# Three buffers for transposed x and five for the output, in a batched matrix product

## The chip, the cores and the metric

The kernel runs on one core of a Trainium2 chip. The metric is the device time of one execution in microseconds (us), less is better; eight runs of the kernel before are shown. One further view is the profile of one execution: its span runs from the first to the last instruction, and its own time is given beside it.

## The reference

32 independent products of a 256x512 matrix by a 512x384 matrix, inputs and output in float32:

```python
def reference(x, y):            # x: 32 x 256 x 512, y: 32 x 512 x 384
    return np.einsum('bij,bjk->bik', x, y).astype(np.float32)
```

x is 16.8 MB, y is 25.2 MB, the output is 12.6 MB: 54.5 MB pass between memory and the core in each execution, whatever the order.

## The kernel before

The 32 products are cut into 8 groups of 4 (`Q = 4`); n numbers the groups from 0 to 7. The product is made in float16 with float32 sums. The work of one group consists of these parts, named by the letters of the text `PLAN`:

- **x**n and **y**n: the loads, issued by SP. x arrives as one transfer of 2 MB, y as one of 3 MB; y7 comes in four quarters. `x_pool` and `y_pool` hold two buffers each, so x(n) waits until VectorE has read x(n-2), and y(n) until it has read y(n-2).
- **T**n: VectorE casts x to float16 (`x_r`, one buffer, line 100) and transposes it in 32x32 blocks into `xt_sb` (line 107: two instructions per group, four for groups 6 and 7).
- **R**n: VectorE casts y to float16 in four pieces (line 113).
- **M**n: TensorE, 128 matmuls in two halves of 64 (line 126). A half fills four PSUM tiles; the pool has eight, so each half of M(n) needs the four tiles of the same half of M(n-1) to have been copied out.
- **C**n and **D**n: the copies from PSUM to the output tile `o_sb` (line 147), by ScalarE (C) and VectorE (D). For groups 0 to 5 ScalarE makes 28 copies and VectorE 4, the last four of the group; for group 6 ScalarE makes all 16 (of 64 partitions), for group 7 the two share 8 and 8.
- **S**n: the store, issued by SP (line 156); for groups 6 and 7 in two halves, here called S6a, S6b, S7a, S7b.

`PLAN` writes the parts out in program order, and `keep_in_program_order` makes each engine follow it. SP, too, issues its transfers in that order: a transfer whose condition isn't met holds up those behind it.

```python
PLAN = """
x0 x1 y0
T0 x2 y1
T1 R0 M0 C0 x3 y2
T2 D0 R1 M1 C1 x4 y3 S0
T3 D1 R2 M2 C2 x5 y4 S1
T4 D2 R3 M3 C3 x6 y5
T5 D3 R4 M4 C4 x7 y6 S2
T6 D4 R5 M5 C5 y7
T7 D5 R6 M6 C6 R7 M7 C7 D7 S3 S4 S5 S6 S7
"""
```

VectorE thus does, for a middle group, T(n), D(n-2), R(n-1). With two buffers of `xt_sb`, the transposes of T(n) write where M(n-2) reads, so they wait for the end of M(n-2), and D(n-2) and R(n-1) stand behind them. With six buffers of `o_sb`, the copies of group 6 wait for the store S0 and those of group 7 for S1.

Of the kernel before, what the change touches and what calls it, by code (L numbers as in the profile page):

```python
# [1 line left out]

# [4 lines left out]


MM_DT = mybir.dt.float16
F32 = mybir.dt.float32  # L10
P = 128


Q = 4
STEP = 4
O_BUFS = 6
WIDE_GROUPS = 6


# [15 lines that stand above are left out]
@with_exitstack  # L35
def kernel(
    ctx: ExitStack,
    tc: tile.TileContext,
    x: bass.AP,
    y: bass.AP,  # L40
    out: bass.AP,
):
    nc = tc.nc

    B, I, J = x.shape
    _, _, K = y.shape

    PQ = P // Q
    R = I // PQ
    T = J // PQ  # L50
    TW = T // 2
    NE = I // P
    N = B // Q

    x_pool = ctx.enter_context(tc.tile_pool(name="x_pool", bufs=2))
    y_pool = ctx.enter_context(tc.tile_pool(name="y_pool", bufs=2))
    xr_pool = ctx.enter_context(tc.tile_pool(name="xr_pool", bufs=1))
    xt_pool = ctx.enter_context(tc.tile_pool(name="xt_pool", bufs=2))
    yr_pool = ctx.enter_context(tc.tile_pool(name="yr_pool", bufs=2))
    o_pool = ctx.enter_context(tc.tile_pool(name="o_pool", bufs=O_BUFS))  # L60
    psum_pool = ctx.enter_context(
        tc.tile_pool(name="psum", bufs=2 * Q, space=bass.MemoryType.PSUM)
    )

    keep = tc.keep_in_program_order

    x_of, y_of, xt_of, yr_of, ps_of, o_of = {}, {}, {}, {}, {}, {}  # L70

    def width(n):
        return PQ if n < WIDE_GROUPS else 2 * PQ

    def on_vector(n, e, g):
        if n < WIDE_GROUPS:
            return (e, g) == (NE - 1, Q - 1)
        return n == N - 1 and g % 2 == 1

    def load_x(n):  # L80
        x_of[n] = x_pool.tile([P, R, J], F32, name="x_sb")
        keep(
            nc.sync.dma_start(
                out=x_of[n],
                in_=x[n * Q : (n + 1) * Q].rearrange("g (p r) j -> (g p) r j", r=R),
            )
        )

    def load_y(n):
        y_of[n] = y_pool.tile([P, T, K], F32, name="y_sb")  # L90
        src = y[n * Q : (n + 1) * Q].rearrange("g (q t) k -> (g q) t k", t=T)
        step = STEP if n == N - 1 else T
        for a in range(0, T, step):
            keep(nc.sync.dma_start(out=y_of[n][:, a : a + step], in_=src[:, a : a + step]))

    def transpose_x(n):


        x_r = xr_pool.tile([P, R, J], MM_DT, name="x_r")
        keep(nc.vector.tensor_copy(x_r, x_of.pop(n)))  # L100
        xt_of[n] = xt_pool.tile([P, NE, TW, P], F32, name="xt_sb")
        b = width(n) // PQ
        src = x_r.bitcast(F32).rearrange("p (b h e) (q t) -> p b e t h q", b=b, e=NE, t=TW)
        dst = xt_of[n].rearrange("p e t (h s b) -> p b e t h s", s=PQ, b=b)
        for e in range(NE):
            for c in range(b):
                keep(nc.vector.transpose(dst[:, c, e], src[:, c, e]))  # L107

    def round_y(n):
        y_sb = y_of.pop(n)  # L110
        yr_of[n] = yr_pool.tile([P, T, K], MM_DT, name="y_r")
        for a in range(0, T, STEP):
            keep(nc.vector.tensor_copy(yr_of[n][:, a : a + STEP], y_sb[:, a : a + STEP]))  # L113

    def multiply(n):
        xt = xt_of.pop(n).bitcast(MM_DT).rearrange("p e t (m c) -> p e t m c", c=2)
        y_r = yr_of.pop(n)
        o_of[n] = o_pool.tile([P, R, K], F32, name="o_sb")
        for e in range(NE):
            for g in range(Q):  # L120
                ps_of[n, e, g] = psum_pool.tile([P, K], F32, name="o_ps")
            for t in range(T):
                for g in range(Q):
                    s = slice(g * PQ, (g + 1) * PQ)
                    keep(
                        nc.tensor.matmul(  # L126
                            ps_of[n, e, g],
                            xt[s, e, t // 2, :, t % 2],
                            y_r[s, t],
                            start=(t == 0),  # L130
                            stop=(t == T - 1),
                        )
                    )

    def collect(n, vector):
        w = width(n)
        per = P // w
        copy = nc.vector.tensor_copy if vector else nc.scalar.copy
        o = o_of[n].rearrange("p (u f) k -> p u f k", u=Q // per)
        for e in range(NE):  # L140
            for g in range(Q):
                if on_vector(n, e, g) != vector:
                    continue
                ps = ps_of.pop((n, e, g))
                a = g % per * w
                for h in range(per):
                    keep(copy(o[a : a + w, g // per, h * NE + e], ps[h * w : (h + 1) * w]))  # L147

    def store(n):
        w = width(n)  # L150
        per = P // w
        o = o_of.pop(n).rearrange("p (u f) k -> p u f k", u=Q // per)
        for u in range(Q // per):
            b = n * Q + u * per
            keep(
                nc.sync.dma_start(
                    out=out[b : b + per].rearrange("g (s f) k -> (g s) f k", s=w),
                    in_=o[:, u],
                )
            )  # L160

    parts = {
        "x": load_x,
        "y": load_y,
        "T": transpose_x,
        "R": round_y,
        "M": multiply,
        "C": lambda n: collect(n, False),
        "D": lambda n: collect(n, True),
        "S": store,  # L170
    }
    for step in PLAN.split():
        parts[step[0]](int(step[1:]))


# [1 line left out]
_INS = ['x', 'y']  # L177
_OUTS = [((32, 256, 384), 'float32')]


# [23 lines left out]
```

## Time and profile before

| what | value |
|---|---|
| median of 8 runs | 136.37 us (135.37 to 136.85) |
| the profiled execution's own time | 136.85 us |
| its span | 135.1 us |
| VectorE busy | 95.5 us (71%) |
| ScalarE busy | 91.7 us (68%) |
| TensorE matmul busy | 58.7 us (43%), mean granted clock 0.802 |
| moved by the SP queue | 54.53 MB, 95.9% of 16 DMA engines' span |

The profiled execution is the longest of the eight shown, 0.48 us over their median.

Every transfer with the time of its issue and of its landing, both in us from the start of the span (the trace gives issue and time to landing; the sum is the landing). A transfer has landed when its last DMA engine is done:

| transfer | issued | landed | | transfer | issued | landed |
|---|---|---|---|---|---|---|
| y1 | 11.2 | 33.8 | | y6 | 84.6 | 103.1 |
| x3 | 17.1 | 38.7 | | S2 | 85.1 | 106.9 |
| y2 | 24.4 | 45.9 | | y7, first quarter | 99.0 | 108.7 |
| x4 | 27.9 | 51.2 | | y7, second | 99.4 | 110.6 |
| y3 | 39.7 | 59.3 | | y7, third | 100.0 | 112.5 |
| S0 | 40.7 | 62.9 | | y7, fourth | 100.7 | 114.3 |
| x5 | 41.9 | 67.9 | | S3 | 101.4 | 117.9 |
| y4 | 54.2 | 75.2 | | S4 | 102.1 | 121.6 |
| S1 | 55.2 | 78.8 | | S5 | 115.4 | 125.2 |
| x6 | 56.4 | 83.7 | | S6a | 122.6 | 127.0 |
| y5 | 69.9 | 90.9 | | S6b | 124.6 | 130.5 |
| x7 | 72.1 | 95.8 | | S7a | 128.5 | 132.3 |
| | | | | S7b | 129.6 | 134.0 |

How to read it: a row of the page's strip has 40 slices of the span, with the busy share in tenths. "Idle before" is time in which an engine did nothing, and the name behind the arrow is what ended it. The DMA share is a mean over 16 engines: it can be under one while some of them are still full.

### The profile page before, as it was taken

How to read it: one execution, taken by the hardware profiler on the slowest of the kernel's cores; microseconds unless marked ns; L12 is line 12 of the kernel's file. 1: busy time of each engine (PE TensorE's matmuls, PEld its weight loads, DVE VectorE, ACT ScalarE, POOL GpSimd, SP SyncE). 2: the span in 40 equal slices, each digit the busy share in tenths (PEclk: the TensorE clock that was granted, in tenths of full speed). 3: DMA queues.
4: the chain of work that ended last, by engine and by line, in shares of the span. 5: the costliest groups of instructions: out<-in, count | busy, mean ns of one | idle time of the engine just before them, and what ended most of it. 6: DMA issues, size and time to landing. Idle time of an engine off the chain costs nothing.

```text
span 135.1 us, 2452 instructions
## 1 busy us (share of the span) xinstructions
PE 58.7 (43%) x1024; PEld 34.5 (26%) x1024; DVE 95.5 (71%) x92; ACT 91.7 (68%) x193; POOL 0.2 (0%) x4
## 2 busy tenths in 40 slices
PE   0000005970099006970099106930499007977700
PEld 0000003540056004540056003610255004634400
DVE  0049999649993899629993899769990999904530
ACT  3000000099997999499986999799958999599720
POOL 0000000000000000000000000000000000000000
PEclk9999999999559955599559955995558965899965
DMA  5999999999999999999999999999999999998774
GB/s 121 422 442 454 408 434 422 442 458 391 456 434 398 429 425 446 346 423 439 444 451 393 418 452 420 444 400 446 449 415 403 404 424 440 422 434 353 313 306 171
DMA packets 4187, 54.68 MB, mean 405 GB/s; under 512 B 464, under 2 KB 464, under 8 KB 1488
## 3 DMA queue, kind: packets, MB, share of 16 engines
q1 hardware_dynamic: 4176, 54.53, 95.9%
q8 instruction: 8, 0.13, 0.4%
q14 instruction: 3, 0.02, 0.0%
HBM read 41.94 MB, written 12.58 MB: 404 GB/s over the span
## 4 chain that ended last, share of the span: by engine, by line
DVE 43%; PE 39%; DMA 6%; ACT 5%; issue 3%; DVEq 0%
PE o_ps L126 39%; DVE xt_sb L107 23%; DVE o_sb L147 11%; DMA x_sb<-in_x_dram 6%; DVE y_r L113 5%; ACT o_sb L147 5%; DVE x_r L100 3%; DVEq L199 0%
## 5 line engine op out<-in xcount | busy, mean ns | idle before, releaser
L147 ACT COPY o_sb<-o_ps 32x384 f32<-32x384 f32 (+1 forms) x192 | 90.4, 471 | 36.8 <-PE o_ps L126 32.7
L126 PE MATMUL o_ps<-y_r,xt_sb 32*128 32x384 f16 x1024 | 58.7, 394 | 68.6 <-DVE y_r L113 66.8
L126 PEld LDWEIGHTS <-xt_sb 32*128 32x128 f16 x1024 | 34.5, 112 | 92.5 <-issue 57.8
L107 DVE STREAM_TRANSPOSE xt_sb<-x_r 128x1024 f32<-128x1024 f32 (+1 forms) x20 | 31.5, 1621 | 16.7 <-PE o_ps L126 16.7
L113 DVE CAST y_r<-y_sb 128x1536 f16<-128x1536 f32 x32 | 28.4, 953 | 0.2
L100 DVE CAST x_r<-x_sb 128x4096 f16<-128x4096 f32 x8 | 18.3, 2288 | 9.7 <-DMA x_sb<-in_x_dram 9.7
L147 DVE COPY o_sb<-o_ps 32x384 f32<-32x384 f32 (+1 forms) x32 | 17.8, 556 | 7.5 <-PE o_ps L126 6.9
L147 ACT ACT_TABLE_LOAD x1 | 1.3, 1283 | 0.7 <-PEq L188 0.7
L188 POOL MEMSET const-bfloat16-1.0<- 128x1 bf16 x1 | 0.1, 103 | 0.0
L188 POOL MEMSET const-uint8-127<- 128x1 uint8 x1 | 0.1, 102 | 0.0
L188 POOL MEMSET const-float32-0.0<- 128x1 f32 x1 | 0.1, 100 | 0.2 <-issue 0.2
L188 POOL MEMSET const-float32-1.0<- 128x1 f32 x1 | 0.1, 99 | 0.0
## 6 DMA issues: line engine op xcount, KB each, us to landing
y_sb<-in_y_dram SPq DMA_DIRECT2D x7, 3072.0 KB, 21.0
x_sb<-in_x_dram SPq DMA_DIRECT2D x8, 2048.0 KB, 22.5
out_dram<-o_sb SPq DMA_DIRECT2D x6, 1536.0 KB, 20.6
y_sb<-in_y_dram SPq DMA_DIRECT2D x4, 768.0 KB, 11.8
out_dram<-o_sb SPq DMA_DIRECT2D x4, 768.0 KB, 4.4
```

The costliest lines, as they stand in the source:

```text
L100: keep(nc.vector.tensor_copy(x_r, x_of.pop(n)))
L107: keep(nc.vector.transpose(dst[:, c, e], src[:, c, e]))
L113: keep(nc.vector.tensor_copy(yr_of[n][:, a : a + STEP], y_sb[:, a : a + STEP]))
L126: nc.tensor.matmul(ps_of[n, e, g], xt[s, e, t // 2, :, t % 2], y_r[s, t], start=(t == 0), stop=(t == T - 1),)
L147: keep(copy(o[a : a + w, g // per, h * NE + e], ps[h * w : (h + 1) * w]))
L188: nc = _bacc.Bacc("TRN2", target_bir_lowering=False, num_devices=1)
```

## The change

Two numbers. The pool of transposed x gets a third buffer, the pool of output tiles loses its sixth. No instruction is added, removed or moved on any engine. With three buffers T(n) waits for the end of M(n-3) in place of M(n-2). With five output buffers, the copies of group 5 wait for S0, those of group 6 for S1, those of group 7 for S2.

```diff
-O_BUFS = 6
+O_BUFS = 5
...
-    xt_pool = ctx.enter_context(tc.tile_pool(name="xt_pool", bufs=2))
+    xt_pool = ctx.enter_context(tc.tile_pool(name="xt_pool", bufs=3))
```

## The prediction

> **What bounds the kernel now.** I read the strip of slices and the queues first, then VectorE's waits, then ScalarE's order of time, and last the transfers of the end.
>
> The page's strip and its queues:
>
> ```profile
> DMA  5999999999999999999999999999999999998774
> GB/s 121 422 442 454 408 434 422 442 458 391 456 434 398 429 425 446 346 423 439 444 451 393 418 452 420 444 400 446 449 415 403 404 424 440 422 434 353 313 306 171
> ...
> q1 hardware_dynamic: 4176, 54.53, 95.9%
> q8 instruction: 8, 0.13, 0.4%
> ```
>
> From the second slice to the 36th, 3 to 121 us, the DMA engines are full at some 425 GB/s; only the last four slices show room. The table of transfers says the same: landings follow each other in the order of issue, at distances that are the sizes over one rate. S0 to x5 is 5.0 us for 2.10 MB, x5 to y4 7.3 us for 3.15 MB, y4 to S1 3.6 us for 1.57 MB: 420 to 437 GB/s. Every one had been issued 8 us or more before its predecessor landed, S0 to y7 alike. The transfers are one line that never runs dry up to S4 at 121.6 us; an earlier issue lengthens the line and lands nothing earlier.
>
> VectorE's waits:
>
> ```profile
> DVE xt_sb L107 <- PE o_ps L126: 16.7, 6, 3.8
> DVE x_r L100 <- DMA x_sb<-in_x_dram: 9.7, 2, 8.5
> DVE o_sb L147 <- PE o_ps L126: 6.9, 2, 5.3
> ```
>
> The first row is the wait at issue: six transposes, T2 to T7, wait 16.7 us in all for the matmuls two groups earlier, at most 3.8 us each.
>
> ScalarE in order of time (start, duration, idle before):
>
> ```profile
> 86.31 13.56 ACT L147 COPY o_sb<-o_ps 32x384 f32<-32x384 f32 x28 [0.63 <-PE o_ps L126]
> 101.79 13.56 ACT L147 COPY o_sb<-o_ps 32x384 f32<-32x384 f32 x28 [1.92 <-PE o_ps L126]
> 116.71 9.80 ACT L147 COPY o_sb<-o_ps 64x384 f32<-64x384 f32 x20 [1.35 <-issue]
> 127.25 1.95 ACT L147 COPY o_sb<-o_ps 64x384 f32<-64x384 f32 x4 [0.74 <-PE o_ps L126]
> ```
>
> A block is the 28 copies of a group, 13.56 us. The idle times before blocks 1 to 5 are 0.94, 1.79, 1.57, 0.63 and 1.92, together 6.85 us: behind VectorE stands an engine with much less room than 16.7 us.
>
> The end, in stretches (columns: length, then busy time and count for PE, weight loads, VectorE, ScalarE, GpSimd; clock, DMA share, GB/s):
>
> ```profile
> 118.00:121.40 3.40, 2.45 (x55) 1.35 (x51) 0.07 (x1) 3.28 (x8) 0.00 (x0) 1.00 1.00 417
> 121.40:125.00 3.60, 2.77 (x64) 1.64 (x60) 1.55 (x3) 3.47 (x8) 0.00 (x0) 1.00 0.88 370
> 125.00:129.00 4.00, 2.35 (x57) 1.44 (x49) 2.34 (x5) 3.17 (x8) 0.00 (x0) 1.00 0.65 260
> 129.00:135.10 6.10, 0.00 (x0) 0.00 (x0) 0.56 (x1) 0.19 (x1) 0.00 (x0) 0.53 0.64 262
> ```
>
> Up to 134.0, the last landing, the 16 engines are idle for a mean of 0.12x3.60 + 0.35x4.00 + (5.0 - 0.64x6.10) = 0.43 + 1.40 + 1.10 = 2.9 us. Those engines wait for S6 and S7, which are issued late because the copies are late. But the last landing is that of the slowest engine. The transfers between 126 and 130 us, in steps of 0.1 us:
>
> ```profile
> GB/s 246 614 184 553 184 369 553 471 492 369 369 246 492 123 307 246 246 184 0 62 61 61 61 61 0 61 0 61 0 0 61 0 61 799 184 492 430 430 492 123
> ...
> q8 instruction: 1, 0.02, 1.6%
> ```
>
> From 127.9 to 129.3 one packet (61 GB/s is 6 KB in 0.1 us) follows another: nearly all engines have run dry and one still works on S6b. In the same stretch stands one packet of instructions, 1.6% of 16 engines for 4 us, so 1.0 us of one engine. Since S4, landings follow at 3.6 (S5), 1.8 (S6a), 3.5 (S6b), 1.8 (S7a) and 1.7 us (S7b). A half store takes 1.8; S6b took 1.7 us more, though it was issued at 124.6, 2.4 us before S6a landed. S7a was issued at 128.5, again before S6b landed. So the slowest engine had work all the time: in this execution the end was set by its line of transfers, lengthened by 1.7 us, and not by the copies.
>
> **The change, part by part.**
>
> The third xt buffer. All six waits go. T2 starts at 27.9 in place of 29.83; D0 and R1 behind it come 1.9 us earlier. What is late next: the second half of M1 needs the PSUM tiles of M0's second half, which ScalarE copies until 40.69, so M1 still ends near 44. The gain reaches ScalarE only as its idle time: 0.94 us before block 1. After that blocks 2 to 4 can follow each other: 27.13 + 4x13.56 = 81.4 for block 4, in place of 86.31. It also needs y4, landed 75.2, plus 6 us (cast 1.0, then half of M4, 4.2 to 5.3 between M and C in the rows), 81.2. From there the loads decide. x6 lands at 83.7; cast 2.29, transposes 4.03 and D4 2.26 bring R5 to 92.3 (before 95.38). Its first piece 0.97, wake-up 0.14 and the half of M5 5.3: block 5 starts at 98.7 and ends at 112.3 in place of 115.36. Block 6 follows at once: 112.3 in place of 116.71, 4.4 us earlier. The y7 quarter that landed at 114.3 ends its cast at 115.3; M7's halves are freed by block 6, so C7, D7 and the issues of S6a, S6b, S7a, S7b come 4.4 us earlier: 118.2, 120.2, 124.1, 125.2. S5 is issued at 112.3.
>
> What that is worth: the line of transfers from S4, landed 121.6, then never runs dry on any engine. S5 125.2, S6a 127.0, S6b 128.8, S7a 130.6, S7b 132.4. Before, 134.0. The gain is 1.6 us if the extra at S6b goes, and 0 if the instruction packet again delays the engine that ends last, since that engine never had a gap to close. The busy shares give a farthest bound of 2.9 us, if all 16 engines end together.
>
> Is the packet's engine fixed? No row tells. I take the value without the repeat, since a full line leaves only the slowest engine's bad luck to matter, and since the profiled run, 0.48 over the median, looks like one with the delay. Both ends stay in the range. The sum: 136.85 - 1.6 = 135.25. Against the median this is a gain of 1.1 us: without the delay, a run of before would be held by the copies instead (S7b issued 129.6 plus 3.5 to 4.0 us), about 0.5 us lower than the profiled one, which is where the median lies.
>
> The Trainium skill, "Perfetto Trace Analysis", section "Optimization Strategy", says that the same gap repeated on the engine that should be saturated can mean too few buffers for the next tile. VectorE's six gaps fit, and by that reading alone the sum would be 136.85 - 16.7 = 120.2; the filled DMA rows contradict it. "DMA: Bandwidth & Descriptors", section "Where 436 GB/s comes from", puts the ceiling of the 16 ports at 435.2 GB/s: my estimate from it is 54.53 MB / 435.2 = 125.3 us for the transfers alone, which speaks against any large gain; the sum by it would end no earlier than about 127 us, and the measured distances of landings are what I use.
>
> The output buffer. C5 newly waits for S0, landed 62.9, and starts no earlier than 98: slack 35 us. C6 waits for S1 (78.8) and starts at 112: slack 33. C7 and D7 wait for S2, landed 106.9; they start at about 118: slack 11 us. S2 stands behind y6 on SP's queue, and y6 is issued earlier, not later. The DVE copy D5 waits for S0 as well, with R6, R7 and D7 queued behind it: it too is 35 us clear. Cost 0; if S2's cover were gone, C7, M7's PSUM and S7 would slip by whatever S2 exceeded 118.
>
> SP's queue: x4 and later loads are issued up to 5 us sooner, none behind a new wait. TensorE: M stays in bursts at clock 0.5 to 1.0; both halves of M7 at the slow rate (a half took 2.8 us in the tail at clock 1.00, 5.3 in M5) would add 5.0 us to S7b, which would be issued at 130.2, still before its turn in the line at 130.6.
>
> **The rivals.**
>
> 1. The delay recurs: the slowest engine ends at 134.0 again. For: it was full throughout. Against: eight instruction packets over 16 engines need not fall there. Time 136.4 to 136.85.
> 2. The copies were the true bound: the end moves with them by 4.4 us, to 132.4. For: the chain of waits ends in matmuls and copies. Against: S5, S6b and S7a landed at the pace of the line, not of their issue.
> 3. Slower: instruction packets fall twice on the engine that ends last, in place of once. Its price is 1.0 us by the row above, at the last store: 137.9. It decides from the second packet on; with only the one it is rival 1. For: nothing but chance and a line without gaps in which to catch up. Against: the number of instructions is unchanged.
>
> **How the numbers follow.** Forecast 0.50 (own range 134.4 to 135.7), rival 1 0.34, rival 2 0.03, rival 3 0.09, the rest, unnamed losses, 0.04. The median moves by over 0.5%, 0.68 us, in the forecast and rival 2: faster 0.52 with a little taken for gains that come out small; rival 1 is within 0.5%, 0.36; slower 0.12. A difference of 0.5% is about what a measurement of this kernel can tell from none. The range, 134.2 to 136.9, takes in the forecast and rival 1, and most of the 2.9 us bound.
>
> **What would show it.** VectorE's wait of line 107 for TensorE gone; ScalarE's idle before blocks 1 to 5 down from 6.85 to 2 us or less; VectorE's wait for x landings up from 9.7; landings up to S4 within 0.5 us of the table; S7b issued near 125 and landing some 7 us later; DMA share near 1 until 130. I am wrong if landings before S4 move, if a copy waits for a store, or if the last landing stays at 134.

## The result, and the profile after

The changed kernel is faster: ratio to the kernel before 0.9942, with a 95% interval of 0.9917 to 0.9968. Its median is 135.25 us (135.07 to 135.93, 12 runs), against 136.21 us for the kernel before in the same comparison (135.19 to 137.63, 33 runs). The ratio is taken over fast runs alone (those not over 1.5% above the fastest of their kernel); the quotient of the two medians is 0.993. The profiled execution took 135.93 us at a span of 134.1 us, against 136.85 and 135.1.

The page's strip and queues of the changed kernel:

```profile
DMA  5999999999999999999999999999999999999991
GB/s 112 420 435 445 432 418 430 459 432 403 452 413 447 403 449 425 355 425 419 474 408 393 435 449 452 423 403 435 427 440 401 409 425 443 420 414 423 417 385 55
...
q1 hardware_dynamic: 4176, 54.53, 96.5%
```

The room in the last four slices (8, 7, 7, 4 before) is gone: the engines are full to the 39th slice. The stretches of the end (length, busy time and count of PE, weight loads, VectorE, ScalarE, GpSimd; clock, DMA share, GB/s):

```profile
121.40:125.00 3.60, 1.86 (x45) 1.08 (x37) 1.93 (x5) 2.79 (x7) 0.00 (x0) 1.00 0.97 404
125.00:129.00 4.00, 0.00 (x0) 0.00 (x0) 0.47 (x1) 0.10 (x1) 0.00 (x0) 0.58 1.00 418
129.00:134.10 5.10, 0.00 (x0) 0.00 (x0) 0.00 (x0) 0.00 (x0) 0.00 (x0) 0.50 0.38 159
```

Between 125 and 129 us the DMA share is 1.00 where it was 0.65, while no matmul is left and hardly a copy: the computation is over and the stores are still draining.

The waits of the changed kernel, all engines:

```profile
DVE x_r L100 <- DMA x_sb<-in_x_dram: 19.8, 5, 8.6
...
DVE y_r L113 <- DMA y_sb<-in_y_dram: 3.2, 4, 0.9
```

The row of the transposes waiting for TensorE (16.7 us before) has no successor here. In its place VectorE waits 19.8 us for x, where it was 9.7, and 3.2 us for y, which it never waited for before. ScalarE in order of time:

```profile
27.04 54.32 ACT L147 COPY o_sb<-o_ps 32x384 f32<-32x384 f32 x112 [25.04 <-PE o_ps L126]
82.51 13.56 ACT L147 COPY o_sb<-o_ps 32x384 f32<-32x384 f32 x28 [1.15 <-PE o_ps L126]
99.03 23.38 ACT L147 COPY o_sb<-o_ps 32x384 f32<-32x384 f32 x48 [2.95 <-issue]
123.16 1.95 ACT L147 COPY o_sb<-o_ps 64x384 f32<-64x384 f32 x4 [0.74 <-PE o_ps L126]
```

The blocks of groups 0 to 3 follow each other without a gap (112 copies in 54.32 us); the gaps that are left stand before group 4 and group 5, where the loads are late. The last copies on ScalarE start 4.1 us earlier, 123.16 for 127.25. And the last store, issue and then time to landing:

```profile
125.54 0.42 SPq L156 DMA_DIRECT2D out_dram<-o_sb  x1
```

```profile
out_dram<-o_sb SPq DMA_DIRECT2D x1, 768.0 KB, 7.6
```

The same store in the kernel before:

```profile
129.63 0.33 SPq L156 DMA_DIRECT2D out_dram<-o_sb  x1
```

```profile
out_dram<-o_sb SPq DMA_DIRECT2D x1, 768.0 KB, 4.4
```

S7b is issued 4.1 us earlier and takes 7.6 us to land, where it took 4.4. Of 4.1 us that the copies won, the end keeps 0.9 (133.1 for 134.0).

### The profile page after: what moved, and what is told of

It reads as the page before. It is cut to its first block, busy times and chain, and to the rows that moved or that the text cites. A ratio compares the mean times of both kernels' runs of the same rounds, so it can differ in the third digit from the quotient of the medians.

```text
span 134.1 us, 2449 instructions
## 1 busy us (share of the span) xinstructions
PE 61.5 (46%) x1024; PEld 35.4 (26%) x1024; DVE 96.3 (72%) x92; ACT 91.7 (68%) x193; POOL 0.2 (0%) x4
## 4 chain that ended last, share of the span: by engine, by line
DMA 42%; DVE 20%; PE 16%; ACT 13%; issue 1%; DVEq 0%
DMA x_sb<-in_x_dram 42%; PE o_ps L126 16%; ACT o_sb L147 13%; DVE xt_sb L107 7%; DVE x_r L100 7%; DVE o_sb L147 5%; DVE y_r L113 1%; DVEq L199 0%; DVEq L100 0%
## 5 line engine op out<-in xcount | busy, mean ns | idle before, releaser
L126 PE MATMUL o_ps<-y_r,xt_sb 32*128 32x384 f16 x1024 | 61.5, 400 | 61.7 <-DVE y_r L113 49.3
L126 PEld LDWEIGHTS <-xt_sb 32*128 32x128 f16 x1024 | 35.4, 113 | 87.4 <-issue 53.4
L100 DVE CAST x_r<-x_sb 128x4096 f16<-128x4096 f32 x8 | 18.4, 2294 | 19.9 <-DMA x_sb<-in_x_dram 19.8
```

Of the source, the lines that this page charges most:

```text
L126: nc.tensor.matmul(ps_of[n, e, g], xt[s, e, t // 2, :, t % 2], y_r[s, t], start=(t == 0), stop=(t == T - 1),)
```

## The experiments

Two theories are told apart. By the **line theory** the end is the end of one full line of transfers, and what the copies win beyond it waits in that line. By the **copies theory** the end is the last copy plus a fixed time for its store.

### Each half of the change, and fewer output buffers

```diff
# e1: kernel before
-O_BUFS = 6
+O_BUFS = 5
# e2: the change itself
# e3: the change, and
-O_BUFS = 5
+O_BUFS = 4
# e4: the change, and
-O_BUFS = 5
+O_BUFS = 3
```

> Only the second half of the change: two buffers of xt_sb as before, five of o_sb in place of six. Line theory (the one line of transfers sets the end, and the third xt buffer is what keeps it full at the end): the new waits are for stores that landed long ago, S0 at 63, S1 at 79 and S2 at 107 us, against copies that start at 102, 117 and 121: no change, within 0.3% of before, and T2 to T7 still wait 16 to 17 us for TensorE. Rival (the smaller output pool costs or gains something of its own): over 0.5% from before in either direction.

> The whole change once more, beside the others on the same chip. Line theory: 0.4 to 0.9% faster than before, S7b issued near 125.5 and landing 7 to 8 us later, at 133. Rival (the copies set the end): the last landing follows the issue of S7b by under 5 us.

> Three buffers of xt_sb, four of o_sb. C7 and D7 now wait for S3, which landed at 118.6 in the changed kernel, while C7 started at 116: a delay of 2.5 to 3 us, so S7b is issued near 128.5 in place of 125.5. Line theory: S7b's turn in the line begins only near 131.3, so the time is that of the change, within 0.3%. Copies theory: the whole delay shows, 2 to 2.5% slower than the change.

> Three buffers of xt_sb, three of o_sb. C6 waits for S3 (landed 118.6, C6 started 112.6) and C7 for S4 (122.2): the copies of group 6 are late by 6 us, those of group 7 by 6 to 7, S7b is issued near 132. Line theory: the slack of the copies, about 5 us, is used up, and the end slips by what exceeds it and the 3.5 us that a half store takes from issue to landing: last landing 135 to 136, 1 to 2% slower than the change, about 1% slower than before. Copies theory: 6 us, 4.5% slower than the change. If the output buffers never matter: equal to the change.

| run | median us | ratio to before | interval | S7b issued | S7b landed |
|---|---|---|---|---|---|
| e1, five output buffers alone | 136.33 | 0.9984 | 0.9946 to 1.0022 | 129.6 | 133.6 |
| e2, the change | 135.32 | 0.9931 | 0.9900 to 0.9961 | 124.8 | 132.6 |
| e3, xt three, output four | 135.34 | 0.9911 | 0.9883 to 0.9939 | 124.5 | 132.6 |
| e4, xt three, output three | 140.15 | 1.0277 | 1.0237 to 1.0317 | 133.0 | 137.0 |

e1: no effect of the output half shows, within 0.4% either way; S7b is issued at 129.56, where it was 129.63, and VectorE's wait stays:

```profile
DVE xt_sb L107 <- PE o_ps L126: 16.4, 6, 3.7
```

e1 and e3 together put the gain on the third xt buffer: with it, five and four output buffers are equal within their intervals. (Three xt and six output buffers together were not run; e9 below has the gain with six output buffers.)

In e3 the wait that I expected didn't appear. I had taken C7 to start at 116, but ScalarE is busy with group 6 until about 119.4, and S3 landed at 118.1. So e3 says nothing on the slack of the copies.

e4 does, though its wait fell earlier than I had put it. With three buffers C5 waits for S2, which landed at 106.5. ScalarE in e4:

```profile
82.54 13.54 ACT L147 COPY o_sb<-o_ps 32x384 f32<-32x384 f32 x28 [2.17 <-issue]
106.56 23.34 ACT L147 COPY o_sb<-o_ps 32x384 f32<-32x384 f32 x48 [10.48 <-DMA out_dram<-o_sb]
```

Its gap of 10.48 us ends with a store. Group 5 starts at 106.56, against 98.33 in e2, 8.2 us late; S7b is issued 8.2 us late too, and the last landing is only 4.4 us late (137.0 for 132.6), the time 4.8. The change thus has some 3.8 us in which copies may be late at no cost, which is 132.6 less the 124.8 of the issue and the 4.0 that S7b needs when only S7a is ahead of it. Neither theory's own number (1 to 2%, or 4.5%) was met against the change, 3.6%: there is slack, as the line theory has it, but 3.8 us of it in place of about 5, and the delay was larger than I had worked out.

### A store less, more copies

In e5 and e6 one store is never issued, in the changed kernel and in the kernel before; in e7 and e8 eight copies of group 6 are made twice.

```diff
# e5 (change), e6 (before): in store(n)
+        if n == 3:
+            return
# e7 (change), e8 (before): in collect(n, vector)
-                for h in range(per):
+                for h in range(per) if (n, e) != (6, 0) else [*range(per)] * 2:
```

> The changed kernel with the store S3 left out: the output of group 3 is never written, so 1.57 MB less pass through the line, 3.6 us by the distances of landings; every copy is still made. Line theory: S7b, issued near 125.5, gets its turn at 127.7 in place of 131.3; the last landing comes 3 to 3.6 us earlier, 2.2 to 2.7% faster than the change, about 3% faster than before. Copies theory: nothing changes, since no copy waits for S3.

> The kernel before with the store S3 left out (the output of group 3 is never written). Here S7b is issued at 129.6 and cannot land before about 133.3, whatever the line. Line theory with the copies just behind: 0 to 0.9 us faster than before, at most 0.7%, a quarter or less of what the same cut gives the changed kernel. If the line alone had set the end of before: 3 us or more, over 2%.

> The changed kernel with the eight copies of the first half of group 6 on ScalarE made twice, 8 x 0.475 = 3.8 us more ahead of S6 and S7. Line theory: S7b is issued near 129.3, still before its turn at 131.3: the time stays within 0.4% of the change. Copies theory: 3.8 us, 2.8% slower than the change.

> The kernel before with the same eight copies made twice. Both theories: the copies have no slack here, S7b is issued near 133.4 and lands near 137.2: 3 to 3.8 us, 2.2 to 2.8% slower than before. Under 1 us would mean that before was bound by the line alone, and that copies had slack without the third buffer too.

| run | median us | ratio to before | interval |
|---|---|---|---|
| e5, change without S3 | 132.26 | 0.9694 | 0.9626 to 0.9762 |
| e6, before without S3 | 136.20 | 0.9994 | 0.9954 to 1.0034 |
| e7, change, eight more copies | 136.66 | 1.0043 | 1.0000 to 1.0086 |
| e8, before, eight more copies | 140.89 | 1.0314 | 1.0241 to 1.0386 |

e5 and e6 are the same cut, 1.57 MB, and settle the case. The changed kernel gains 3.0 us by it (132.26 for the 135.25 of the change; by the ratios, 0.9694 for 0.9942 or 0.9931, 3.2 to 3.4 us), nearly the 3.6 us that the bytes take in the line; no gain of the kernel before shows (0.9994, within 0.4%). The kernel before was held by its copies, the changed one by the line. In e5 the copies are the bound again: S7b, issued at 125.41, lands 4.0 us later.

e8: with no slack, the eight copies cost 4.3 us by the profiles (last landing 138.4 for 134.0) and 4.6 us, 3.1%, in the runs, more than their own 3.8 us. e7 missed its expectation: 1.0 to 1.1% slower than the change (1.0043 over 0.9942 or 0.9931), in place of 0.4% at most. S7b is issued at 129.82, 5.0 us later than in e2, and lands 4.0 us later, so the copies have overtaken the line. The excess over 3.8 us comes from TensorE. ScalarE, which in the changed kernel and in e2 goes from group 6 into group 7 without a gap (48 copies in one piece), waits for TensorE in between:

```profile
124.64 1.93 ACT L147 COPY o_sb<-o_ps 64x384 f32<-64x384 f32 x4 [1.14 <-PE o_ps L126]
```

The stretches of e7 beside those of the changed kernel above:

```profile
118.00:121.40 3.40, 1.78 (x24) 1.04 (x27) 0.00 (x0) 3.26 (x8) 0.00 (x0) 0.51 0.99 419
121.40:125.00 3.60, 3.60 (x55) 2.05 (x48) 0.27 (x1) 2.39 (x6) 0.00 (x0) 0.52 0.98 411
```

Between 118 and 125 the granted clock is 0.51 and 0.52, where the changed kernel had 1.00 from 121.4 to 125: the delayed first half of M7 fell into a stretch of half clock. In e8, too, the granted clock is 0.50 from 125 to 129, with 59 matmuls in these 4.0 us, and S7b's issue is 4.8 us late. A delay of the copies is not added as it is; it can move matmuls to another clock.

### Another order in place of another buffer, two stores less, half the copies

```diff
# e9: kernel before, two xt and six output buffers; X(n) is the cast of x, T(n) now only the transposes
-T2 D0 R1 M1 C1 x4 y3 S0
+X2 D0 R1 T2 M1 C1 x4 y3 S0
...
# e10: the change, in store(n)
+        if n in (3, 4):
+            return
# e11: the change, in collect(n, vector)
-                for h in range(per):
+                for h in range(per) if (n, e) != (6, 0) or g > 1 else [*range(per)] * 2:
```

> The kernel before, two buffers of xt_sb and six of o_sb, with another order on VectorE: the cast of x(n), then D(n-2), R(n-1), and only then the transposes of x(n), whose wait for M(n-2) is over by then. Nothing is added. Line theory (any way of taking VectorE's wait out of the copies' chain ends at the same line): the same gain as the change, 0.4 to 0.9% faster than before; S7b is issued between 123 and 126. Rival (the third buffer itself brings something, such as the earlier transposes): no gain over before, or clearly less than the change.

> The changed kernel with the stores S3 and S4 left out (groups 3 and 4 of the output are never written), 3.15 MB less in the line. Two-bound theory: leaving out S3 alone gave 3.0 us and brought the line's end to 129.4, the 4.0 us that S7b needs from its issue at 125.4; now the copies are the bound and the second store left out gives under 0.6 us more: 131.7 to 132.4 us. If the line alone counted: another 3.6 us, 128.6.

> The changed kernel with four copies of group 6 made twice on ScalarE, 1.9 us ahead of S6 and S7, half of what cost the change 1.0 to 1.2%. Two-bound theory: S7b issued near 127.4, plus 4.0 is 131.4, still before the line's end at 132.6 to 133.1: within 0.3% of the change, 0.3 to 0.9% faster than before. Copies theory: 1.9 us, 0.8% slower than before.

| run | median us | ratio to before | interval | S7b issued | S7b landed |
|---|---|---|---|---|---|
| e9, reordered | 135.34 | 0.9948 | 0.9924 to 0.9972 | 123.3 | 132.4 |
| e10, change without S3 and S4 | 131.90 | 0.9712 | 0.9656 to 0.9768 | 124.8 | 128.8 |
| e11, change, four more copies | 135.29 | 0.9942 | 0.9913 to 0.9972 | 126.6 | 132.6 |

All three came out as expected by the two-bound theory: the line bounds the changed kernel, and the copies are the next bound. e9 takes VectorE's wait away without a buffer. Its copies come earlier than the change's:

```profile
25.91 67.95 ACT L150 COPY o_sb<-o_ps 32x384 f32<-32x384 f32 x140 [23.91 <-PE o_ps L129]
96.74 23.39 ACT L150 COPY o_sb<-o_ps 32x384 f32<-32x384 f32 x48 [2.88 <-PE o_ps L129]
```

Five blocks without a gap, and S7b issued 1.6 us before e2's; the time is the same, because the line ends at the same place. So no gain of the third buffer shows beside the end of the wait.

e10: the second store left out is worth 0.4 us by the medians (131.90 for 132.26) after the 3.0 us of the first, and nothing by the ratios (0.9712 for 0.9694), which do not tell the two apart. The copies are the bound, as in e5 (S7b, issued at 124.78, again lands 4.0 us later). e11: S7b, 1.8 us later than in e2, lands at the same 132.6, and the ratio is the change's own.

## Why the prediction was right, and where it was not

**The time.** 135.25 us was forecast and measured, the direction too; against the measured ratio, 0.58%, the forecast gain of 1.1 us in 136.37 (0.8%) is a little large. That the time was met to the hundredth is luck: the sum took 1.6 us off the profiled execution, and from profile to profile the gain was 0.9 (135.93 for 136.85).

**The line.** Right. The landings up to S4 kept their places although loads were issued up to 6.5 us sooner (y5 63.4 for 69.9): S4 landed at 122.2 in the profiled execution and 121.6 in e2, against 121.6 before. The sign "within 0.5 us of the table" holds in e2 and is missed by a little in the profiled execution, where the landings from x5 to S4 come 0.6 us later. After S4 the halves follow at 1.8 to 1.9 us. S7b was put at 125.2 for its issue and 132.4 for its landing; it was 125.5 and 133.1, and 124.8 and 132.6 in e2. "DMA: Bandwidth & Descriptors" of the Trainium skill, section "Where 436 GB/s comes from", gives a ceiling of 435.2 GB/s; from y3 to S4 the changed kernel landed 26.7 MB in 62.8 us, 426 GB/s, just under that ceiling. The same section says that between the chip's memory (HBM) and the core's own (SBUF) some 358 GB/s is the limit; the 426 GB/s measured here are above that, and the measurement decides.

**The copies.** Right within 1.1 us: ScalarE's group 4 at 81.4 (measured 82.51), group 5 at 98.7 (99.03), group 6 at 112.3 (S5, the store behind group 5, was issued at 112.6). One entry of the list of signs was wrong by its own terms: idle time before blocks 1 to 5 "down to 2 us or less". My own starts left 98.7 - (81.4 + 13.56) = 3.7 us before group 5; measured 1.15 + 2.95 = 4.1.

**The output buffer.** Right: no cost shows (e1), with slack that ends between four buffers and three (e3, e4).

**The step that failed: "in this execution the end was set by its line of transfers ... and not by the copies".** For the slowest DMA engine of that one execution it can be read from the table, where S7a and S7b follow the late S6b at 1.8 and 1.7 us, the pace of the line; but it is not what bounds the kernel before. e6 refutes it as a rule: with 3.6 us taken out of the line, the time does not move. The end before was S7b's issue plus 4.0 us, 129.6 + 4.0 = 133.6, with some 0.4 us more in the profiled execution; the line alone would have ended 0.5 to 1.0 us sooner, at 132.6 to 133.1, where it ends in e2 and in the changed kernel. e1, issued within 0.1 us of before at the end, shows the schedule of before without most of the delay: S6b lands 2.4 us behind S6a, and the end is 133.6, S7b's issue plus 4.0.

I had read the late landing of S6b as the slowest engine's bad luck. It was more regular than that. In four profiles whose line had run short at that place, S6b landed well behind S6a, where a half store is 1.8: 3.5 us in before, 3.9 in e4, 3.9 in e8 and 3.8 in e10. It is not there each time: e1 has 2.4 us and e7 2.3. The times to landing of S6a, S6b and S7b in e8, in this order (size, then us from issue):

```profile
out_dram<-o_sb SPq DMA_DIRECT2D x1, 768.0 KB, 3.3
...
out_dram<-o_sb SPq DMA_DIRECT2D x1, 768.0 KB, 5.2
...
out_dram<-o_sb SPq DMA_DIRECT2D x1, 768.0 KB, 4.0
```

In the changed kernel S6b lands 1.8 us after S6a, as a full line has it, and 1.8 to 1.9 in e2, e3, e9 and e11: with a full line no such delay shows. So rivals 1 and 3, which left its return to chance alone, missed that it goes with a short line, if not every time. Rival 2, "The copies were the true bound", had the right bound for the kernel before and was given 0.03; its price, the whole 4.4 us, left out that the line ends only 0.5 to 1.0 us sooner. The gain against the median came out near because the prediction also held the other account, "a run of before would be held by the copies instead, S7b issued 129.6 plus 3.5 to 4.0 us", which is what e1, e5, e8 and e10 measured as 4.0. The true sum: bound by the copies before, 133.6 to 134.0; bound by the line after, 132.6 to 133.1; the difference 0.5 to 1.4 us around the measured 0.8 (0.58% of 136.2).

**The slack of the copies.** The forecast of a slow M7 left S7b's issue 5.4 us of room, from 125.2 to its turn at 130.6. That was too much: 3.8 by e2 and e4, since the last store needs 4.0 us even with only S7a ahead of it.

**The rule of repeated gaps.** "Perfetto Trace Analysis" of the Trainium skill, section "Optimization Strategy", says that a gap repeated on the engine that should be saturated can mean too few buffers. Here VectorE, with its six gaps, was not the engine that set the time. There were too few buffers, and filling the gaps by a buffer (e2) or by another order (e9) both worked; but 16.7 us of gaps were worth 0.8 us of time.

## What to carry to other kernels

When a wait goes, ask what the next bound is and where it ends, not how long the wait was: here copies came 4 us earlier and the line of transfers let 0.8 us through. Two bounds that end within a microsecond of each other are told apart by taking work from one alone: the same store left out gave 3.0 us in one kernel and nothing in the other. And a line that is full by its mean share shows its slack only at its end; compare the issue and the landing of the last transfer.

## What the runs showed of the hardware

A store of 0.79 MB takes 3.3 us from issue to landing with nothing ahead of it (S6a and S7a in e8 and e10), of which the bytes at the line's pace are 1.8. S6b, issued 2.0 us behind S6a, should by this take 3.3 - 2.0 + 1.8 = 3.1 us, and takes 5.1 to 5.2 there, 2.0 us more. One packet of instructions (16 KB, some 1.0 us of one engine) stands in that stretch of before and may have a part in it. But between 126 and 130 us e1 has one as well, and there S6b is only 0.6 us late (2.4 for 1.8). No run moved the packet away, so the reason is open. The granted clock changed the price of a delay: 3.8 us of copies cost 5.0 us at S7b's issue in e7, when half of M7 fell into half clock.
